# Decoder layer with 32 routed experts: transposes moved into the next expert's first product, the residual split around a product, the overflow branch placed at expert 23

## The chip, the cores and the metric

The kernel runs on one core of one Trainium2 chip. The metric is the device time of one execution in microseconds (us). Of the core's engines this text uses TensorE (PE in the profile, with PEld for its weight loads), VectorE (DVE), ScalarE (ACT), GpSimd (POOL) and SyncE (SP), the queue that issues the large weight transfers.

## What is computed

One decoder layer for 256 tokens of width 1024, in float32: three causal token mixers in parallel, a layer norm, then the part that concerns this change, a top-4-of-32 layer of experts, and a second layer norm on `alpha * x + moe(x)`. The reference, cut to one expert and to the norms:

```python
x = layer_norm(alpha * x + mix(x), ln1_g, ln1_b)

def expert_block(args):
    xb, e = args
    hid = xb @ w_gate_up[e] + b_gate_up[e]          # 1024 -> 2048
    glu = jnp.minimum(hid[:, :D_FF], SWIGLU_LIMIT)
    lin = jnp.clip(hid[:, D_FF:], -SWIGLU_LIMIT, SWIGLU_LIMIT)
    act = glu * jax.nn.sigmoid(SWIGLU_ALPHA * glu) * (lin + 1.0)
    return act @ w_down[e] + b_down[e]              # 1024 -> 1024
...
y = jnp.zeros((t + 1, d)).at[tok_pad].add(y_pad * gate_pad[:, None])[:t]
x = layer_norm(alpha * x + y, ln2_g, ln2_b)
```

Each expert's weights are 12 MB (8 MB up, 4 MB down), so all 32 have to be read once, whatever the routing is.

## The kernel before

After the mixers and the first norm the kernel runs a loop over the experts (line 1317). The first product of expert e, the second product of expert e-1 and the scatter of expert e-2 are written in iteration e, and a scheduler then sets the order of each engine from this program order, the dependences and its own estimates, so that parts of neighbouring iterations can be woven into each other. Only a conditional is a border that nothing is moved over.

**Weights.** `load(e)` issues, on SP's queue, eight pieces of 1 MB for the up weights `wu` of expert e and four for the down weights `wd` of expert e-1. They land in a ring of buffers of 1 MB; a piece can be issued when the product that last used its buffer is done.

**Gather.** Every second iteration `gather` (line 1139) makes the tokens of two experts, `xg`, by 16 matmuls `ps_xg` (line 1152) of one-hot columns `g` with the normed tokens `x`; ACT and DVE copy them out with the gain and shift of the first norm. `spread` (line 1259, POOL) makes `sel`, with which a bias row is added by a matmul.

**First product.** `gemm1` (lines 1163 to 1183) adds the bias to two PSUM tiles `pg` and `pl` (line 1167), then runs over eight pieces k, each four matmuls (line 1171); the scatter of expert e-2 is written behind k = 0. DVE and ACT make `el` from `pg` and `pl` (`eg`, `es` and `el`, lines 1178 to 1182).

**Second product.** `gemm2` (lines 1185 to 1214) transposes `el` in four 128 x 128 blocks (`pt`, line 1188), ACT copies these to `aT` (line 1190); DVE makes the one-hot `gg`, PE transposes it and multiplies it with the gates (`pq`, lines 1197 and 1199), DVE copies `gT` and `gs` out (lines 1203 and 1205). Then comes the bias of `po` (line 1201) and 16 matmuls with the four down pieces (line 1208). ACT makes `oh` and DVE `ol` from `po`, scaled by `gs`.

**Scatter.** `scatter` (lines 1217 to 1224) adds `oh` and `ol`, through `gT`, into four PSUM tiles `y`, which stay open over the whole loop: four matmuls with `oh`, four with `ol`.

**Residual.** The term `alpha * x` of the second norm, with x the output of the first norm, is put into the same four tiles by `residual(h)`, h = 0 and 1 for the halves of the width, in iterations 5 and 6. `lnr` holds the four rows of norm parameters in 32 partitions. `ln_row` spreads a row of it over 128 partitions by four matmuls (`ps_ln`, line 1245); DVE makes `res` from the gain row (line 1234), then adds the shift row (line 1236), and two matmuls with `ident` add `res` into `y` (line 1238). `ps_l` rows of the same form (line 1245) are made for the second norm in the last iterations.

**Conditional.** `IFAT` is 13: in that iteration the loads of expert 14 are issued early, the scatter of expert 12 is put ahead, and a conditional follows that handles experts with more than 64 tokens. In the profiled execution its body is not run; its branch is evaluated on each engine's sequencer.

All PSUM tiles of the tag `misc` (`pt`, `pq`, `ps_ln`, half of the `ps_xg`) share one bank, and `eg`, `es`, `aT`, `oh`, `ol` and `res` share three SBUF buffers of the tag `e3`.

Of the kernel before, what the change touches and what calls it, by code (L numbers as in the profile page):

```python
# [8 lines left out]
F32 = mybir.dt.float32  # L9
# [4 lines left out]
OP = mybir.AluOpType  # L14
# [3 lines left out]
P = 128  # L18
# [5 lines left out]
NRAW, NHL, NA, NB, XB, IFAT, LPP, Y1, Y2, Y3, SG, MG = 3, 3, 4, 3, 1, 13, 1, 3, 3, 3, 4, 2  # L24
ALPHA = 2 ** 0.25
# [8 lines left out]
def tile_layer(ctx, tc, x, xT, memT, w_in, w_convT, a_log, dt_bias, gdn_norm_w, w_mem_kv, w_p_gdn, w_p_sb,  # L34
               w_p_mem, w_o, ln1_g, ln1_b, ln1_T, w_router, b_router, w_gate_up, b_gate_up, w_down, b_down,
               ln2_g, ln2_b, out, dbg=None, cap=CAP, nexp=NE):
    nc = tc.nc
# [15 lines left out]
    V = {}  # L53
# [862 lines left out]
    def begin_gates():  # L916
# [10 lines left out]
        for n, v in enumerate((ln1_g, ln1_b, ln2_g, ln2_b)):  # L927
            nc.gpsimd.dma_start(lnr[8 * n:8 * n + 8, :], v.rearrange("(q c) -> q c", q=8))

# [203 lines left out]
    XG, ACT, SEL, YO = {}, {}, {}, {}  # L1133
# [29 lines left out]
    def gemm1(e, sel, between=None):  # L1163
# [5 lines left out]
        for k in range(KT):  # L1169
# [3 lines left out]
            if k == 0 and between:  # L1173
                between()
# [10 lines left out]
    def gemm2(e, sel, rc, gates):  # L1185
# [14 lines left out]
        po = psg.tile([P, 512], F32, name=f"po{e}", tag="o")  # L1200
        nc.tensor.matmul(po, sel, bias[:, 2, :], start=True, stop=False)  # L1201
# [3 lines left out]
        nc.vector.tensor_copy(gs, pq[:, T:T + 1])  # L1205
        for ft in range(8):
# [18 lines left out]

    def residual(h):

        hs = slice(512 * h, 512 * h + 512)
        res = [ew.tile([P, 512], F32, name=f"res{i}{h}", tag="e3", bufs=3) for i in range(2)]
        for n in range(2):  # L1230
            ps = ln_row(n, h, f"ps_ln{h}{n}")
            for i in range(2):
                if n == 0:
                    nc.vector.scalar_tensor_tensor(res[i], x1[:, i, hs], ALPHA, ps, op0=OP.mult, op1=OP.mult)
                else:
                    nc.vector.scalar_tensor_tensor(res[i], ps, ALPHA, res[i], op0=OP.mult, op1=OP.add)
        for i in range(2):
            nc.tensor.matmul(yps[i][h], ident, res[i], start=False, stop=False, skip_group_check=True)
# [34 lines left out]
    def further_slots():  # L1273
# [16 lines left out]
        with tc.For_i(0, -(-T // cap) - 1, 1):  # L1290
            with tc.For_i(0, nexp, 1) as er:
# [18 lines left out]
                gemm2("o", osel, rc, [gc[:, i:i + 1] for i in range(2)])  # L1310
# [6 lines left out]
    for e in range(nexp + 1):  # L1317
# [3 lines left out]
        if e < nexp:  # L1321
# [3 lines left out]
            gemm1(e, SEL[e], (lambda: scatter(e - 2)) if e - 2 in YO else None)  # L1325
        elif e - 2 in YO:
            scatter(e - 2)
        if e == 1:
            gates_of()
        if e in (5, 6):  # L1330
            residual(e - 5)
        if e == nexp - 1:
            ln2 = ln2_rows()
        if e:
            gemm2(e - 1, SEL[e - 1], rank[:, :, e - 1], [G[:, i, e - 1:e] for i in range(2)])
# [64 lines left out]
```

## Time and profile before

| | us |
|---|---|
| median of three executions | 1317.63 (1315.15 to 1318.44) |
| the profiled execution | 1317.42 |
| its span in the trace | 1315.7 |
| PE busy | 1247.6 (95% of the span) |
| PE weight loads busy | 681.7 (52%) |
| DVE, ACT, POOL busy | 404.3, 278.1, 100.2 |

The span is the time from the first to the last recorded instruction; the profiled execution's own time is 1.7 us longer. Times in the trace are us from the span's start. In the page's table of 40 slices each slice is 32.9 us; the experts begin around the 11th. A row of the timeline gives start, length, engine, line, operation, output and inputs and how many in a row, and in brackets how long the engine had been idle and what released it. Weight loads and matmuls of a float32 product are each recorded as two passes, so the 16 matmuls of a second product appear as 32.

### The profile page before, as it was taken

What the parts mean: (1) busy time and instruction counts of PE and PEld (TensorE: products, weight loads), DVE (VectorE), ACT (ScalarE), POOL (GpSimd) and SP (SyncE); (2) the same over time, 40 slices, a digit from 0 to 9 for tenths busy, and PEclk for the clock granted to TensorE, in tenths of its full rate; (3) what the DMA queues carried; (4) which work ended last, traced back from release to release, by engine and by line L of the source; (5) the groups of instructions that cost most, each with busy time, mean ns of one, the idle gap of its engine ahead of it and who ended that gap; (6) DMA issues with size and microseconds to landing.
All of it is one profiled execution on the core that took longest, in us unless ns stands there. A gap on an engine that the chain in (4) does not pass through costs nothing. (4 is left out here: it accounts for less than half of the span.)

```text
span 1315.7 us, 16784 instructions
## 1 busy us (share of the span) xinstructions
PE 1247.6 (95%) x7023; PEld 681.7 (52%) x7023; DVE 404.3 (31%) x696; ACT 278.1 (21%) x448; POOL 100.2 (8%) x155
## 2 busy tenths in 40 slices
PE   8999999999999998899999999999999999999995
PEld 7998889999734434333333344333333333333342
DVE  6865646557412112111111221111121111111113
ACT  5665636445301101010101011010101011010111
POOL 5223323001000000000000000000000000000001
PEclk9999999999999998799999999999999999999998
DMA  7632347858699999899999979999999999999991
GB/s 241 193 128 89 105 163 232 283 184 300 257 416 423 424 421 425 340 411 407 421 424 421 404 290 422 424 423 422 424 422 425 423 421 424 421 422 425 423 414 49
DMA packets 117135, 453.54 MB, mean 345 GB/s; under 512 B 7440, under 2 KB 47456, under 8 KB 84288
## 3 DMA queue, kind: packets, MB, share of 16 engines
q1 hardware_dynamic: 116096, 450.39, 85.3%
q0 software_dynamic: 960, 2.04, 0.6%
q8 instruction: 57, 0.93, 0.3%
q14 instruction: 22, 0.18, 0.0%
HBM read 451.35 MB, written 1.05 MB: 344 GB/s over the span
## 5 line engine op out<-in xcount | busy, mean ns | idle before, releaser
L1171 PE MATMUL pg<-wu,xg 128*64 128x512 f32 x1024 | 283.6, 600 | 0.0
L1171 PE MATMUL pl<-wu,xg 128*64 128x512 f32 x1024 | 277.8, 593 | 0.0
L1208 PE MATMUL po<-wd,aT 128*64 128x512 f32 x1024 | 240.3, 608 | 0.0
L1178 DVE TENSOR_SCALAR eg<-pg 128x512 f32<-128x512 f32 x32 | 22.1, 692 | 431.9 <-PE pg L1171 431.9
L1171 PEld LDWEIGHTS pl<-wu,xg 128*64 128x64 f32 x1024 | 77.3, 137 | 146.3 <-issue 146.3
L1171 PEld LDWEIGHTS pg<-wu,xg 128*64 128x64 f32 x1024 | 70.5, 136 | 126.5 <-issue 111.6
L1208 PEld LDWEIGHTS po<-wd,aT 128*64 128x64 f32 x1024 | 67.7, 138 | 113.3 <-issue 107.4
L68 ACT ACTIVATE es<-eg 128x512 f32<-128x512 f32 x32 | 20.2, 632 | 463.3 <-DVE eg L1178 463.3
L1214 DVE SCALAR_TENSOR_TENSOR ol<-po,gs,oh 128x512 fp32r<-128x512 f32 x32 | 24.0, 751 | 189.8 <-ACT oh L1213 189.6
L1259 POOL CAST sel<-brs 128x128 fp32r<-128x128 f32 x32 | 11.9, 373 | 880.7 <-PE po L1201 880.1
L1152 PEld LDWEIGHTS ps_xg<-g,x 128*128 128x128 f32 x512 | 61.5, 196 | 28.3 <-issue 27.6
L1152 PE MATMUL ps_xg<-g,x 128*128 128x128 f32 x512 | 68.1, 286 | 0.2 <-DVE g L1141 0.2
L1213 ACT ACTIVATE oh<-po,gs 128x512 fp32r<-128x512 f32 x32 | 22.0, 687 | 218.3 <-PE po L1208 218.3
L1159 ACT ACTIVATE xg<-ps_xg,l1T 128x128 f32<-128x128 f32 x64 | 29.3, 458 | 137.8 <-PE ps_xg L1152 122.4
L1161 DVE TENSOR_SCALAR xg<-ps_xg,l1T 128x128 f32<-128x128 f32 x64 | 26.2, 410 | 90.4 <-ACT xg L1159 89.6
L1223 PE MATMUL y<-oh,gT 64*128 64x512 f32 x128 | 33.8, 461 | 18.8 <-ACT oh L1213 18.0
L1223 PEld LDWEIGHTS y<-oh,gT 64*128 64x128 f32 x128 | 13.3, 184 | 62.0 <-ACT oh L1213 36.5
L1188 PEld LDWEIGHTS pt<-ident,el 128*128 128x128 f32 x128 | 14.4, 146 | 29.2 <-issue 18.1
L1223 PE MATMUL y<-ol,gT 64*128 64x512 f32 x128 | 27.1, 412 | 0.2
L1179 DVE TENSOR_SCALAR el<-pl 128x512 f32<-128x512 f32 x32 | 22.1, 692 | 5.0 <-PE pl L1171 5.0
L1188 PE MATMUL pt<-ident,el 128*128 128x128 f32 x128 | 22.2, 296 | 0.7
L1167 PE MATMUL pl<-bias,sel 128*128 128x512 f32 x32 | 15.7, 492 | 7.2 <-DVE el L1179 7.2
(578 smaller groups left out, 1730.8 us busy)
## 6 DMA issues: line engine op xcount, KB each, us to landing
wu<-in_w_gate_up_dram SPq DMA_DIRECT2D x256, 1024.0 KB, 19.0
wd<-in_w_down_dram SPq DMA_DIRECT2D x127, 1024.0 KB, 19.6
wg<-in_w_in_dram SPq DMA_DIRECT2D x12, 1024.0 KB, 5.8
wo<-in_w_o_dram SPq DMA_DIRECT2D x4, 1024.0 KB, 5.1
wk<-in_w_in_dram SPq DMA_DIRECT2D x2, 1024.0 KB, 6.1
wv<-in_w_in_dram SPq DMA_DIRECT2D x2, 1024.0 KB, 6.0
wsq<-in_w_in_dram SPq DMA_DIRECT2D x2, 1024.0 KB, 5.1
wsk<-in_w_in_dram SPq DMA_DIRECT2D x2, 1024.0 KB, 5.1
```

The lines of the kernel that those rows point to most:

```text
L68: o = nc.scalar.activation(out, in_, func, **kw)
L1152: nc.tensor.matmul(ps[:, k, :], x1[:, i, d * P:(d + 1) * P], g2[:, i].rearrange("p a b -> p (a b)"), start=(i == 0), stop=(i == 1))
L1159: nc.scalar.activation(dst, ps[:, k, :], AF.Identity, scale=g, bias=b)
L1161: nc.vector.tensor_scalar(dst, ps[:, k, :], g, b, op0=OP.mult, op1=OP.add)
L1171: nc.tensor.matmul(ps[64 * h:64 * h + 64, :], XG[e][:, k, :], WU[e][k][:, 512 * c:512 * c + 512], start=False, stop=(k == KT - 1))
L1178: nc.vector.tensor_scalar(g, pg, 7.0, None, op0=OP.min)
L1179: nc.vector.tensor_scalar(l, pl, 7.0, -7.0, op0=OP.min, op1=OP.max)
L1188: nc.tensor.transpose(pt[:, j, :], ACT[e][:, j * P:(j + 1) * P], ident)
L1208: nc.tensor.matmul(po[64 * h:64 * h + 64, :], aT[:, ft % 4, ft // 4, :], WD[e][ft // 2].rearrange("p (a c) -> p a c", a=2)[:, ft % 2, 512 ...
L1213: nc.scalar.activation(oh, po, AF.Copy, scale=gs)
L1214: nc.vector.scalar_tensor_tensor(ol, po, gs, oh.bitcast(F32), op0=OP.mult, op1=OP.subtract)
L1223: nc.tensor.matmul(yps[i][h], gT[64 * h:64 * h + 64, i, :], o[64 * h:64 * h + 64, :], start=(e == 0 and n == 0), stop=(e == nexp - 1 and n ...
```

## The change

- `IFAT` is 23 instead of 13: the early loads, the early scatter and the conditional move to iteration 23.
- The transposes of `el`, the copy `aT`, the transposes `pq` and the copies `gT` and `gs` leave `gemm2` and become `turned(e)`. It is called for expert e-1 within the first product of expert e, behind k = 1; the scatter of expert e-2 stays behind k = 0.
- The residual is split. `residual(h)`, now called ahead of the first product in iterations 5 and 7, makes only the gain row and `res = alpha * x * gain`. `add_residual(h)`, called behind that first product, adds the shift row directly into `y`, by eight matmuls of a new constant `al` (a column of `ident` times alpha, made once on POOL) with `lnr`, and then adds `res` as before.
- The gate values (`gates_of`) are made in iteration 0 instead of 1.

PE, in the gathering iteration of two woven experts, around the second product of the expert before (the rows `po` with `wd`). Before, from the bias of the next first product on:

```order
L1167 MATMUL pg_5438<-bias,sel_5436 128x512
L1167 MATMUL pl_5439<-bias,sel_5436 128x512
L1197 MATMUL pq_5350<-ident,gg_5351 128x128 x2
L1199 MATMUL pq_5350<-G,gg_5351 128x1 x2
L1208 MATMUL po_5357<-wd_0_5281,aT_5348 64x512 x4
L1152 MATMUL ps_xg_5410<-g_12_5407,x_2139 128x128 x7
L1208 MATMUL po_5357<-wd_1_5283,aT_5348 64x512 x4
L1152 MATMUL ps_xg_5410<-g_12_5407,x_2139 128x128
L1208 MATMUL po_5357<-wd_2_5285,aT_5348 64x512 x4
L1188 MATMUL pt_5490<-ident,el_5337 128x128 x4
L1208 MATMUL po_5357<-wd_3_5287,aT_5348 64x512 x4
```

The gather, `pq` and `pt` all stand within the second product. After, the same place:

```order
L1169 MATMUL pg_5442<-bias,sel_5440 128x512
L1169 MATMUL pl_5443<-bias,sel_5440 128x512
L1215 MATMUL po_5365<-wd_0_5285,aT_5320 64x512 x4
L1191 MATMUL pt_5462<-ident,el_5359 128x128 x4
L1215 MATMUL po_5365<-wd_1_5287,aT_5320 64x512 x4
L1215 MATMUL po_5365<-wd_2_5289,aT_5320 64x512 x4
L1215 MATMUL po_5365<-wd_3_5291,aT_5320 64x512 x4
```

Only `pt` of the following expert has stayed there. What left it stands within the first product of the same pair (rows `pg` and `pl` with `wu`), between its pieces. After:

```order
L1230 MATMUL y_3824<-ol_5266,gT_5211 128x512
L1200 MATMUL pq_5322<-ident,gg_5323 128x128 x2
L1173 MATMUL pg_5295<-wu_1_5271,xg_5148 64x512 x2
L1173 MATMUL pl_5296<-wu_1_5271,xg_5148 64x512 x2
L1202 MATMUL pq_5322<-G,gg_5323 128x1 x2
L1212 MATMUL po_5365<-bias,sel_5175 128x512
L1154 MATMUL ps_xg_5414<-g_12_5411,x_2139 128x128 x3
L1173 MATMUL pg_5295<-wu_2_5273,xg_5148 64x512 x2
L1173 MATMUL pl_5296<-wu_2_5273,xg_5148 64x512 x2
L1154 MATMUL ps_xg_5414<-g_12_5411,x_2139 128x128 x5
```

The transposes `pq` now surround piece 1, and the gather's first rows `ps_xg` come behind them and around piece 2.

PE in iteration 5, first half of the residual. Before, behind the last piece of the first product (`wu_7`):

```order
L1171 MATMUL pl_4461<-wu_7_4448,xg_4313 64x512 x2
L1167 MATMUL pg_4625<-bias,sel_4623 128x512
L1167 MATMUL pl_4626<-bias,sel_4623 128x512
L1245 MATMUL ps_ln_4521<-lnr,ident 128x128 x4
L1238 MATMUL y_3819<-res_4512,ident 128x512
L1238 MATMUL y_3821<-res_4513,ident 128x512
L1188 MATMUL pt_4530<-ident,el_4388 128x128 x4
L1197 MATMUL pq_4537<-ident,gg_4538 128x128 x2
L1199 MATMUL pq_4537<-G,gg_4538 128x1 x2
L1208 MATMUL po_4544<-wd_0_4450,aT_4535 64x512 x4
```

The shift row, the two residual matmuls, `pt` and `pq` follow each other between two products. After, within the first product of iteration 5:

```order
L1191 MATMUL pt_4491<-ident,el_4408 128x128 x3
L1248 MATMUL y_3821<-lnr,al 128x128 x4
L1200 MATMUL pq_4498<-ident,gg_4499 128x128 x2
L1202 MATMUL pq_4498<-G,gg_4499 128x1 x2
L1173 MATMUL pg_4471<-wu_2_4440,xg_4315 64x512 x2
L1173 MATMUL pl_4472<-wu_2_4440,xg_4315 64x512 x2
L1248 MATMUL y_3823<-lnr,al 128x128 x4
L1251 MATMUL y_3821<-res_4467,ident 128x512
L1173 MATMUL pg_4471<-wu_3_4442,xg_4315 64x512 x2
L1173 MATMUL pl_4472<-wu_3_4442,xg_4315 64x512 x2
L1251 MATMUL y_3823<-res_4468,ident 128x512
```

The `lnr,al` matmuls and the residual matmuls have moved between the pieces of the product; the gain row `ps_ln` (not among these rows) stands in the second product ahead of it.

The diff, cut to what matters:

```diff
-NRAW, NHL, NA, NB, XB, IFAT, LPP, Y1, Y2, Y3, SG, MG = 3, 3, 4, 3, 1, 13, 1, 3, 3, 3, 4, 2
+NRAW, NHL, NA, NB, XB, IFAT, LPP, Y1, Y2, Y3, SG, MG = 3, 3, 4, 3, 1, 23, 1, 3, 3, 3, 4, 2
...
+        V["al"] = al = ctile([32, 8], "al", pool=mo2)
+        nc.gpsimd.tensor_scalar(al, ident[0:32, 8:16], ALPHA, None, op0=OP.mult)
...
-            if k == 0 and between:
-                between()
+            if k < len(between):
+                between[k]()
...
-    def gemm2(e, sel, rc, gates):
+    def turned(e, rc, gates):
+
         pt = psg.tile([P, 4, P], F32, name=f"pt{e}", tag="misc")
...
-        po = psg.tile([P, 512], F32, name=f"po{e}", tag="o")
-        nc.tensor.matmul(po, sel, bias[:, 2, :], start=True, stop=False)
         gT = ew.tile([P, 2, P], F32R, name=f"gT{e}", tag="gT", bufs=1)
         nc.vector.tensor_copy(gT.rearrange("p i t -> p (i t)"), pq[:, :T])
         gs = ew.tile([P, 1], F32, name=f"gs{e}", tag="gs")
         nc.vector.tensor_copy(gs, pq[:, T:T + 1])
+        TU[e] = aT, gT, gs
+
+    def gemm2(e, sel):
+        aT, gT, gs = TU.pop(e)
+        po = psg.tile([P, 512], F32, name=f"po{e}", tag="o")
+        nc.tensor.matmul(po, sel, bias[:, 2, :], start=True, stop=False)
...
     def residual(h):
 
         hs = slice(512 * h, 512 * h + 512)
-        res = [ew.tile([P, 512], F32, name=f"res{i}{h}", tag="e3", bufs=3) for i in range(2)]
-        for n in range(2):
-            ps = ln_row(n, h, f"ps_ln{h}{n}")
-            for i in range(2):
-                if n == 0:
-                    nc.vector.scalar_tensor_tensor(res[i], x1[:, i, hs], ALPHA, ps, op0=OP.mult, op1=OP.mult)
-                else:
-                    nc.vector.scalar_tensor_tensor(res[i], ps, ALPHA, res[i], op0=OP.mult, op1=OP.add)
-        for i in range(2):
-            nc.tensor.matmul(yps[i][h], ident, res[i], start=False, stop=False, skip_group_check=True)
+        ps = ln_row(0, h, f"ps_ln{h}")
+        RES[h] = [ew.tile([P, 512], F32, name=f"res{i}{h}", tag="e3", bufs=3) for i in range(2)]
+        for i in range(2):
+            nc.vector.scalar_tensor_tensor(RES[h][i], x1[:, i, hs], ALPHA, ps, op0=OP.mult, op1=OP.mult)
+
+    def add_residual(h):
+
+        for i in range(2):
+            for q in range(4):
+                r = 4 * h + q
+                nc.tensor.matmul(yps[i][h][:, q * P:(q + 1) * P], V["al"][:, r:r + 1].to_broadcast([32, P]), lnr,
+                                 start=False, stop=False, skip_group_check=True)
+        for i in range(2):
+            nc.tensor.matmul(yps[i][h], ident, RES[h][i], start=False, stop=False, skip_group_check=True)
...
-            gemm1(e, SEL[e], (lambda: scatter(e - 2)) if e - 2 in YO else None)
-        elif e - 2 in YO:
+            if e in (5, 7):
+                residual((e - 5) // 2)
+            between = [lambda: scatter(e - 2)] if e - 2 in YO else []
+            if e:
+                between.append(lambda: turned(e - 1, rank[:, :, e - 1], [G[:, i, e - 1:e] for i in range(2)]))
+            gemm1(e, SEL[e], between)
+            if e in (5, 7):
+                add_residual((e - 5) // 2)
+        else:
             scatter(e - 2)
-        if e == 1:
+            turned(e - 1, rank[:, :, e - 1], [G[:, i, e - 1:e] for i in range(2)])
+        if e == 0:
             gates_of()
-        if e in (5, 6):
-            residual(e - 5)
...
-            gemm2(e - 1, SEL[e - 1], rank[:, :, e - 1], [G[:, i, e - 1:e] for i in range(2)])
+            gemm2(e - 1, SEL[e - 1])
```

## Rows read from the trace of the kernel before

**Rows 1.** Page, parts 1 and 2: engines' busy us; 40 slices, clock in tenths, GB/s.
```profile
PE 1247.6 (95%) x7023; PEld 681.7 (52%) x7023; DVE 404.3 (31%) x696; ACT 278.1 (21%) x448; POOL 100.2 (8%) x155
...
PEclk9999999999999998799999999999999999999998
...
GB/s 241 193 128 89 105 163 232 283 184 300 257 416 423 424 421 425 340 411 407 421 424 421 404 290 422 424 423 422 424 422 425 423 421 424 421 422 425 423 414 49
```

**Rows 2.** Waits of PE, 800 to 1280: us in total, times, longest.
```profile
PE y L1223 <- ACT oh L1213: 11.0, 13, 0.8
PE pl L1167 <- DVE el L1179: 4.1, 14, 0.3
PE pg L1167 <- POOL sel L1259: 1.7, 2, 0.9
```

**Rows 3.** Timeline of PE, the scatters' second halves (others between left out).
```profile
402.97 0.62 PE L1223 MATMUL y<-ol,gT 64*128 64x512 f32 x4
...
428.31 0.63 PE L1223 MATMUL y<-ol,gT 64*128 64x512 f32 x4
...
457.22 0.62 PE L1223 MATMUL y<-ol,gT 64*128 64x512 f32 x4
...
595.28 0.94 PE L1223 MATMUL y<-ol,gT 64*128 64x512 f32 x4
...
622.00 0.95 PE L1223 MATMUL y<-ol,gT 64*128 64x512 f32 x4
...
654.19 0.95 PE L1223 MATMUL y<-ol,gT 64*128 64x512 f32 x4
```

**Rows 4.** Timeline of PE, second products, at 901 and in the last iterations.
```profile
901.17 5.37 PE L1208 MATMUL po<-wd,aT 128*64 128x512 f32 x24
...
1254.12 1.15 PE L1245 MATMUL ps_l<-lnr,ident 32*128 32x128 f32 x8
1255.21 1.94 PE L1208 MATMUL po<-wd,aT 128*64 128x512 f32 x8
```

**Rows 5.** Timeline of PE at the residual's first half.
```profile
500.89 1.25 PE L1245 MATMUL ps_ln<-lnr,ident 32*128 32x128 f32 x8 [1.62 <-DVE res L1234]
...
502.93 3.78 PE L1238 MATMUL y<-res,ident 128*128 128x512 f32 x4 [0.78 <-DVE res L1236]
```

**Rows 6.** Windows: us, busy PE, PEld, DVE, ACT, POOL; PEclk, DMA share, GB/s.
```profile
496.00:504.00 8.00, 4.93 (x20) 2.18 (x17) 5.16 (x8) 0.63 (x1) 0.00 (x0) 0.86 1.01 419
504.00:512.00 8.00, 7.32 (x20) 3.52 (x20) 0.82 (x3) 0.59 (x1) 0.00 (x0) 0.50 1.03 429
544.00:552.00 8.00, 7.11 (x18) 3.84 (x20) 1.58 (x5) 0.59 (x1) 0.00 (x0) 0.50 0.76 323
552.00:560.00 8.00, 8.00 (x28) 2.31 (x26) 0.00 (x0) 0.00 (x0) 0.00 (x0) 0.72 0.52 184
752.00:760.00 8.00, 6.87 (x36) 2.62 (x34) 3.17 (x6) 1.10 (x2) 0.00 (x0) 1.00 0.41 165
760.00:768.00 8.00, 6.58 (x43) 3.69 (x39) 1.94 (x4) 0.85 (x2) 0.00 (x0) 1.00 0.20 61
1288.00:1296.00 8.00, 7.11 (x37) 2.75 (x35) 1.24 (x3) 1.16 (x2) 0.00 (x0) 1.00 0.01 2
```

**Rows 7.** Timeline of PE and of DVE around a first product's end.
```profile
1251.21 0.49 PE L1167 MATMUL pl<-bias,sel 128*128 128x512 f32 x1 [0.30 <-DVE el L1179]
...
1282.78 0.42 DVE L1203 CAST gT<-pq 128x256 fp32r<-128x256 f32 x1 [0.48 <-PE pq L1199]
1283.12 0.68 DVE L1182 TENSOR_TENSOR el<-el,es 128x512 f32<-128x512 f32 x1
```

**Rows 8.** Waits of SP, 735 to 775, and timeline of PE, there and at the end.
```profile
SPq L829 <- PEq L1340: 7.8, 1, 7.8
...
754.81 0.44 PE L1197 MATMUL pq<-ident,gg 128*128 128x128 f32 x2 [1.13 <-ACT aT L1190]
...
1293.83 7.09 PE L1208 MATMUL po<-wd,aT 128*64 128x512 f32 x32
```

More of the change, by code (lines that the diff above doesn't have):

```diff
@@ L1132, in tile_layer @@
     yps = [[psy.tile([P, 512], F32, name=f"y{i}{dh}", tag=f"y{i}{dh}") for dh in range(2)] for i in range(2)]
-    XG, ACT, SEL, YO = {}, {}, {}, {}
+    XG, ACT, SEL, TU, YO = {}, {}, {}, {}, {}
     def load(e):
@@ L1161, in gather, with gemm1 @@
                     nc.vector.tensor_scalar(dst, ps[:, k, :], g, b, op0=OP.mult, op1=OP.add)
-    def gemm1(e, sel, between=None):
+    def gemm1(e, sel, between=()):
         pg = psg.tile([P, 512], F32, name=f"pg{e}", tag="glu")
@@ L1224, in scatter @@
                                      start=(e == 0 and n == 0), stop=(e == nexp - 1 and n == 1), skip_group_check=True)
+    RES = {}
     def residual(h):
         hs = slice(512 * h, 512 * h + 512)
-        res = [ew.tile([P, 512], F32, name=f"res{i}{h}", tag="e3", bufs=3) for i in range(2)]
-        for n in range(2):
-            ps = ln_row(n, h, f"ps_ln{h}{n}")
-            for i in range(2):
-                if n == 0:
-                    nc.vector.scalar_tensor_tensor(res[i], x1[:, i, hs], ALPHA, ps, op0=OP.mult, op1=OP.mult)
-                else:
-                    nc.vector.scalar_tensor_tensor(res[i], ps, ALPHA, res[i], op0=OP.mult, op1=OP.add)
-        for i in range(2):
-            nc.tensor.matmul(yps[i][h], ident, res[i], start=False, stop=False, skip_group_check=True)
+        ps = ln_row(0, h, f"ps_ln{h}")
+        RES[h] = [ew.tile([P, 512], F32, name=f"res{i}{h}", tag="e3", bufs=3) for i in range(2)]
+        for i in range(2):
+            nc.vector.scalar_tensor_tensor(RES[h][i], x1[:, i, hs], ALPHA, ps, op0=OP.mult, op1=OP.mult)
[7 more added lines that the diff above has]
+            nc.tensor.matmul(yps[i][h], ident, RES[h][i], start=False, stop=False, skip_group_check=True)
     def ln_row(n, h, name):
@@ L1309, in further_slots @@
                 WD["o"] = [down_piece("o", k, er) for k in range(4)]
-                gemm2("o", osel, rc, [gc[:, i:i + 1] for i in range(2)])
+                turned("o", rc, [gc[:, i:i + 1] for i in range(2)])
+                gemm2("o", osel)
                 scatter("o")
```

## The prediction

> **What bounds the kernel now.** I read the page first. TensorE (PE) is busy for 95% of the span, and the 40 slices tell the stages apart: from the 12th slice on, the experts, the DMA moves 421 to 425 GB/s in nearly every slice. Two slices stand out: the 17th (340 GB/s), where the granted clock also falls to 0.7, and the 24th (290 GB/s) [rows 1]. In the expert stage PE and DMA are close. Two experts need 24 pieces of 1.049 MB, 25.17 MB, so 59.6 us at 422 GB/s. PE needs 58.9 us, as the marks below show. Which of the two binds is told by the waits: in 480 us of the stage PE waits 11.0 us for the scaled copy `oh`, 4.1 us for `el`, 1.7 us for `sel`, and the list ends there [rows 2]. No weight load of it waits for a DMA. So PE binds, and the pieces arrive just in time.
>
> Next the marks: each end of a scatter on PE is a beat, one expert apart [rows 3]. 402.97 to 428.31 to 457.22 is 25.3 and 28.9 us, 54.3 a pair: experts not woven into each other. 595.28 to 622.00 to 654.19 is 26.7 and 32.2, 58.9 a pair: the woven order of most experts. Between, four beats from 457.22 to 595.28 take 138.1 us. They hold the residual.
>
> **The residual's split.** What would four beats cost without it? The orders around them: 25.3 + 32.2 + 26.7 + 32.2 = 116.4 us. So the residual costs 21.7 us today. What is in that? Its own PE work: a group of eight `ps_l` rows goes from 1254.12 to 1255.21, 1.09 us [rows 4]; four of these are 4.4. The eight residual matmuls took 3.78 us for four at half clock [rows 5], so some 0.45 each at full clock, 3.6 for all eight. Stalls: PE stands 1.62 us before the second row group and 0.78 before the residual matmuls, each for DVE's `res` [rows 5]; twice, 4.8. The rest, 21.7 - 4.4 - 3.6 - 4.8 = 8.9, is the clock: behind the stalls it is granted at 0.50, once for each half (504 to 512 and 544 to 552), and as PE frees slots late, the DMA drops to 323 and 184 GB/s [rows 6].
>
> After the change `ps_ln` is formed once a half and handed to DVE; PE then has pieces k2 and k3 to multiply and the `lnr,al` matmuls to do before it needs `res`, as the order shows. Work: two row groups of 1.09 (2.2), sixteen `lnr,al` matmuls, which are as long as four such groups (4.4), and the same eight residual matmuls (3.6): 10.1. Around each half some four cuts of the product: eight weight-and-multiply steps in a row take 1.94 us and 24 take 5.37 [rows 4], so 0.214 each and 0.22 for a fresh start; eight cuts are 1.6. For waits I leave 2.0, one of the 0.3 to 0.8 us kind per group. That is 13.7 in place of 21.7, **-8.0**. The bounds: nothing of the waits and cuts, -11.6; all the stalls come back but not the clock, -4. I take -8.0, since the stall rows are both waits for DVE work that now runs under 3.5 us or more of product per half.
>
> **Experts not woven** (four at the start, four behind the conditional, before and after alike). The first product of one expert now begins right after the second of another, with the old 0.84-us wait for `sel` [rows 2] covered by the gather or gone; in exchange `pt` and `pq` cut the product at three places, 0.66. About -0.15 each, **-1.2**; bounds 0 and -3 (from -0.84 + 0.44).
>
> **The woven experts**, ten pairs. Per pair PE runs the same matmuls. The second product loses the cuts by the gather and `pq`; the first product gets them: I count nine cuts before and nine after. What could be new is a wait. First, `pt` now stands behind only `pl`'s bias and one down piece (0.49 + 1.94 us) after DVE's first `el` step; DVE needs two more steps of one size, 0.68 each [rows 7], so it is ready with about 1 us to spare: nothing. Second, the gather's `ps_xg` now follows `pq` and waits till DVE has copied `gT` (0.42 [rows 7]) and the one column `gs` out of the same bank, with only a bias matmul (as `pl`'s, 0.49) between: with two hand-overs some 0.2 us per pair. The wait for `oh` (0.84) stays where it is. So **+2.0**; the bounds are cuts saved at two places, -0.4 a pair, and a full copy exposed in both experts, +1.1: -4 to +11.
>
> **The conditional at 23 instead of 13.** On PE its stretch costs 1.13 us, where `pq` waits for the copy `aT` that was just made [rows 8]. After the change `aT` is made during the first product, so this last goes: **-1.0**, bounds 0 and -2.5. The DMA is what suffers: SP drains its queue, waits 7.8 us for PE's branch [rows 8], and the DMA falls to 165 and 61 GB/s [rows 6]; against 422 these are 8 x 0.61 + 8 x 0.86 = 11.7 us of rest. PE did not wait for it. Moving the rest to expert 23 costs nothing if the ring of slots covers it there too. The cover: from the conditional to the end the DMA runs full, 421 to 425 GB/s [rows 1], and yet its last bytes came by about 1288, while the last second product began at 1293.83, took 7.09 [rows 6, 8] and so reached its last quarter 5.3 us later. There is some 11 us of cover left at the end, and the same sum of rests and short beats lies ahead of it after the change. I cost it at nothing; if the cover were gone, it would be +8 to +12.
>
> **The end.** The last first product has the same 1.13-us pattern; **-0.5**.
>
> Sum: -8.0 - 1.2 + 2.0 - 1.0 - 0.5 = -8.7. The profiled execution took 1317.42 us (span 1315.7), 0.2 under the median of 1317.63, so nothing is to be corrected: 1317.4 - 8.7 = **1308.7, said 1309**.
>
> **Rivals.**
>
> R1, slower: the moved transposes expose a wait at every expert. `pt`, its copy `aT`, `pq` and `gT` pass from PE to ACT to PE to DVE to PE, and each hand-over that is not covered is worth what `oh` costs now, 0.84 us [rows 2]. If one such wait appears in each of 28 experts, that is +23.5 against -8.7 and the time is 1332. It decides from 8.7/28 = 0.31 us per expert. For it: four hand-overs lie in one product, and all PSUM tiles named `misc` share one bank. Against it: a down or up piece is 1.9 us, longer than any of the copies, and the order leaves one between nearly all of them.
>
> R2, no change: the clock falls again. The two residual blocks still put transposes, `lnr,al` and `pq` matmuls beside each other, and if the clock drops to half as now, the 8.9 us return: 1317.6. For it: in the trace the fall to 0.50 begins in the stretch with those small matmuls. Against it: the fall stands behind a stretch with only 4.9 of 8 us busy [rows 6], and every later expert has `pt` and `pq` without a fall (from the 19th slice on, 9 throughout [rows 1]).
> The Trainium skill ("TensorE: Matmul & The Clock Gate", section "Part 4: PE-mode transpose") says that transposes do not count as PE activity for the clock the way matmuls do. That speaks against a change that sets transposes beside the residual; by it the time would be R2's, and by the rows of the later experts, with as many transposes and a clock of 1.00, it would be the forecast's. It gives R2 its chance.
>
> R3, cheaper: no new waits, cuts saved, stalls of the residual all gone: -11.6 - 3 - 4 is 1299 at best; I take 1301.
>
> R4, the DMA binds and not PE. Then PE's gains count for nothing and only the DMA's rests do: at the residual 8 x (1 - 323/422) + 8 x (1 - 184/422) = 1.9 + 4.5 = 6.4 us go, the 11.7 at the conditional stay: 1311. For it: the DMA needs 59.6 us a pair, PE 58.9. Against it: [rows 2].
> The skill ("Perfetto Trace Analysis", section "Identifying the Most-Contended Engine") holds that the matmul busy share is a poor measure and the weight loads' share a better one; that share is 52% here [rows 1], which would make the DMA the bound and R4 the answer. The waits of the trace disagree: PE stops for no transfer.
>
> R5: expert 23 has less cover than 13, and PE starves by the rest's 8 to 12 us: 1317 to 1321.
>
> **How the numbers follow.** Chances: the forecast 0.52, R4 0.06 (beside it, 1311), R3 0.13, R2 0.11, R5 0.05, R1 0.13. A measurement of this kernel can tell about 0.3%, 4 us, from no change: faster is below 1313.7, slower above 1321.6. Faster: forecast, R4 and R3 less 0.02 of the forecast's upper edge, 0.69. Same: R2, R5 and that edge, 0.18. Slower: R1, 0.13. The range has to take in R3, the forecast and R2: 1299 to 1319; left out are R1, the dear half of R5 and a little below.
>
> **What would show it.** In the trace of the changed kernel: the four beats around iterations 5 to 8 sum to about 130 us, the granted clock stays near 1.00 there, and the DMA does not fall below 400 GB/s; waits for `res` are under 1 us. The `pt` and `ps_xg` rows of woven experts carry waits of 0 and 0.2 us, and a pair takes 59.1. At expert 23 SP again waits about 8 us for PE's branch, the DMA rests about 12 us and PE's weight loads do not wait. Waits of PE for `aT` or `gT` of 0.3 us and more at each expert would prove R1; a clock of 0.50 in iteration 5 or 7, R2; waits of PE for `wu` or `wd`, R4 or R5.

## The result and the profile after

The changed kernel takes 1331.1 us (median of four, 1329.21 to 1332.9) against 1318.04 for the kernel before on the same chip: 1.0101 times as long, 95% interval 1.0077 to 1.0125. It is 13 us slower, where 9 us faster had been predicted. The profiled execution's span is 1328.9 us.

The page of the changed kernel, parts 1, 2 and 6 (as in [rows 1]; of part 6 the line of the up weights, with KB each and us from issue to landing):

```profile
PE 1262.2 (95%) x7039; PEld 682.1 (51%) x7039; DVE 400.3 (30%) x692; ACT 276.8 (21%) x448; POOL 99.8 (8%) x156
...
PEclk9999999999999999999999999999999999999998
...
GB/s 238 177 142 74 117 135 224 305 191 289 258 418 422 424 422 423 421 413 415 422 420 419 422 424 424 421 423 422 422 423 424 263 389 422 425 421 424 423 278 32
...
wu<-in_w_gate_up_dram SPq DMA_DIRECT2D x256, 1024.0 KB, 10.3
```

The same line of the kernel before:

```profile
wu<-in_w_gate_up_dram SPq DMA_DIRECT2D x256, 1024.0 KB, 19.0
```

The dip of clock and transfers in the 17th slice is gone, and the one of the conditional has moved from the 24th to the 32nd. A piece lands 10.3 us after its issue; before it took 19.0. So fewer pieces are under way at a time, and it is PE that is late.

Waits of PE, 800 to 1280, changed kernel (us in total, times, longest; before: [rows 2]):

```profile
PE y L1230 <- ACT oh L1220: 11.0, 13, 0.8
PE pg L1169 <- PEq L1360: 4.0, 1, 4.0
PE pl L1169 <- DVE el L1181: 3.5, 12, 0.3
PE ps_xg L1154 <- DVE gs L1206: 1.7, 5, 0.3
```

Two of these lines are new: 4.0 us behind the branch, and 0.3 for each gather. (A fifth, `ps_l` with 0.3, belongs to the end, below.) They are far from 13 us. The beats tell the rest. Timeline of PE, changed kernel, scatters (as in [rows 3]):

```profile
406.56 0.62 PE L1230 MATMUL y<-ol,gT 64*128 64x512 f32 x4
...
432.27 0.62 PE L1230 MATMUL y<-ol,gT 64*128 64x512 f32 x4
...
461.55 0.63 PE L1230 MATMUL y<-ol,gT 64*128 64x512 f32 x4
...
592.20 0.95 PE L1230 MATMUL y<-ol,gT 64*128 64x512 f32 x4
...
619.18 0.95 PE L1230 MATMUL y<-ol,gT 64*128 64x512 f32 x4
...
651.80 0.95 PE L1230 MATMUL y<-ol,gT 64*128 64x512 f32 x4
```

With all marks of both traces the span can be cut into stretches that answer to each other:

| stretch (us) | before | after | difference |
|---|---|---|---|
| up to the first mark | 402.97 | 406.56 | +3.6 |
| two beats, not woven | 54.25 | 54.99 | +0.7 |
| four beats with the residual | 138.06 | 130.65 | -7.4 |
| seventeen woven beats | 498.39 | 504.05 | +5.7 |
| five beats around and behind the conditional | 143.04 | 149.37 | +6.3 |
| from the last woven mark to the last mark | 65.83 | 70.10 | +4.3 |
| behind it | 13.16 | 13.18 | 0.0 |

The residual came out as predicted (130.65 against "about 130"), and four other stretches took it back with 17.0 us. The first line of the table is another matter. Up to the first row of the gather (351.80 before, 355.89 after) the programs are the same but for one small POOL instruction; in the traces of the twelve kernels of this study this row begins anywhere from 351.8 to 357.6, and the trace of before is the earliest of them. So the late start is not the change's, and from the gather on the changed kernel is 9.1 us longer in this pair of traces. What is missing to 13 lies with the residual: before, its four beats took 138.06 us in this trace, and the same code took 132.3 to 134.8 in three others (below). Against those the difference would be some 12 to 15 us, an estimate.

The end, timeline of PE, changed kernel, from 1276 on (all of its waits in the last first product, and the first behind it):

```profile
1276.98 0.90 PE L1258 MATMUL ps_l<-lnr,ident 32*128 32x128 f32 x6 [0.34 <-DVE gs L1206]
...
1280.83 0.93 PE L1258 MATMUL ps_l<-lnr,ident 32*128 32x128 f32 x6 [0.68 <-ACT ln L1266]
...
1284.72 0.71 PE L1258 MATMUL ps_l<-lnr,ident 32*128 32x128 f32 x4 [0.68 <-ACT ln L1266]
...
1288.60 0.48 PE L1258 MATMUL ps_l<-lnr,ident 32*128 32x128 f32 x2 [0.68 <-ACT ln L1266]
...
1297.71 0.66 PE L1191 MATMUL pt<-ident,el 128*128 128x128 f32 x4 [0.60 <-DVE el L1184]
```

Before, the `ps_l` rows stood in four whole groups between the down pieces of a second product and waited for nothing [rows 4]. Now they stand behind `pq` in a first product, share its bank, and are cut into pieces of two to six. These rows and the `pt` behind them wait 0.34 + 3 x 0.68 + 0.60 = 3.0 us. One more wait is laid bare: the scatter behind that second product, before and after:

```profile
1264.06 0.73 PE L1223 MATMUL y<-oh,gT 64*128 64x512 f32 x3
```

```profile
1270.05 0.73 PE L1230 MATMUL y<-oh,gT 64*128 64x512 f32 x3 [0.84 <-ACT oh L1220]
```

Before, the last `ps_l` group stood ahead of this scatter, and `oh` was ready when PE came to it. With 3.0 and 0.84 added and the old 1.13 for `aT` gone, waits make up 2.7 of the 4.3 us. The rest is put down to the cuts; that was not measured apart.

### The profile page after: what moved, and what is told of

It reads as the page before. It is cut to its first block, busy times and chain, and to the rows that moved or that the text cites. A ratio compares the mean times of both kernels' runs of the same rounds, so it can differ in the third digit from the quotient of the medians.

```text
span 1328.9 us, 16802 instructions
## 1 busy us (share of the span) xinstructions
PE 1262.2 (95%) x7039; PEld 682.1 (51%) x7039; DVE 400.3 (30%) x692; ACT 276.8 (21%) x448; POOL 99.8 (8%) x156
## 5 line engine op out<-in xcount | busy, mean ns | idle before, releaser
L1173 PE MATMUL pg<-wu,xg 128*64 128x512 f32 x1024 | 316.3, 604 | 0.0
L1173 PE MATMUL pl<-wu,xg 128*64 128x512 f32 x1024 | 306.8, 593 | 0.0
L1215 PE MATMUL po<-wd,aT 128*64 128x512 f32 x1024 | 231.7, 597 | 0.0
L1173 PEld LDWEIGHTS pl<-wu,xg 128*64 128x64 f32 x1024 | 86.6, 137 | 145.8 <-issue 145.7
L1215 PEld LDWEIGHTS po<-wd,aT 128*64 128x64 f32 x1024 | 68.8, 136 | 127.3 <-issue 117.3
L1173 PEld LDWEIGHTS pg<-wu,xg 128*64 128x64 f32 x1024 | 75.7, 136 | 106.0 <-issue 87.5
L1204 DVE CAST gT<-pq 128x256 fp32r<-128x256 f32 x32 | 13.6, 424 | 147.2 <-PE pq L1202 147.2
L1193 ACT COPY aT<-pt 128x512 f32<-128x512 f32 x32 | 18.6, 580 | 46.5 <-PE pt L1191 46.5
L1191 PEld LDWEIGHTS pt<-ident,el 128*128 128x128 f32 x128 | 13.4, 140 | 28.2 <-DVE xg L1163 9.7
## 6 DMA issues: line engine op xcount, KB each, us to landing
wu<-in_w_gate_up_dram SPq DMA_DIRECT2D x256, 1024.0 KB, 10.3
```

The lines of the kernel that those rows point to most:

```text
L1173: nc.tensor.matmul(ps[64 * h:64 * h + 64, :], XG[e][:, k, :], WU[e][k][:, 512 * c:512 * c + 512], start=False, stop=(k == KT - 1))
L1193: nc.scalar.copy(aT.rearrange("p j a b -> p j (a b)"), pt)
L1215: nc.tensor.matmul(po[64 * h:64 * h + 64, :], aT[:, ft % 4, ft // 4, :], WD[e][ft // 2].rearrange("p (a c) -> p a c", a=2)[:, ft % 2, 512 ...
```

## Experiments

The theory after the result: each of the three parts has its own price, the moved transposes and the moved conditional cost, the split gains. The rivals: the DMA paces the pairs (59.60 us, the sum of 26.98 and 32.62, is what 24 pieces need at 422 GB/s); the conditional costs only beside the moved transposes; the split's gain is lost further on. The first four kernels take the parts singly.

**The conditional alone at 23.**

```diff
-NRAW, NHL, NA, NB, XB, IFAT, LPP, Y1, Y2, Y3, SG, MG = 3, 3, 4, 3, 1, 13, 1, 3, 3, 3, 4, 2
+NRAW, NHL, NA, NB, XB, IFAT, LPP, Y1, Y2, Y3, SG, MG = 3, 3, 4, 3, 1, 23, 1, 3, 3, 3, 4, 2
```

> The kernel before with one number changed: the conditional stands at expert 23 instead of 13. Nothing else moves. The changed kernel's trace shows 4.0 us of idle PE behind the branch at 23, where the kernel before showed 0.53 behind the branch at 13, and the six beats around the conditional are 6.3 us longer. Theory A (the later place itself costs, since the code behind the branch or the drained queue is met differently there): about +4 to +6 us on the kernel before, with an idle PE of about 4 us behind the branch. Theory B (the place costs nothing, the moved transposes beside it do): within 1.5 us of the kernel before, idle PE behind the branch 0.5 to 1 us. The prediction's own figure for the move alone was 0, with the DMA's cover as the only danger.

Measured: 1322.68 us, ratio 1.0042 (1.0023 to 1.0062), 5.5 us slower. Timeline of PE at the branch:

```profile
1060.46 0.77 PE L1167 MATMUL pg<-bias,sel 128*128 128x512 f32 x1 [3.57 <-PEq L1340]
```

The five beats there take 148.3 us, 5.3 more than at 13. Theory A so far: the move costs by itself, and not by the transposes.

**The changed kernel with the conditional at 13.** 
```diff
-NRAW, NHL, NA, NB, XB, IFAT, LPP, Y1, Y2, Y3, SG, MG = 3, 3, 4, 3, 1, 23, 1, 3, 3, 3, 4, 2
+NRAW, NHL, NA, NB, XB, IFAT, LPP, Y1, Y2, Y3, SG, MG = 3, 3, 4, 3, 1, 13, 1, 3, 3, 3, 4, 2
```

> The changed kernel with the conditional back at expert 13. Theory A (the later place costs): 4 to 6 us less than the changed kernel, so about 1325 to 1327. Theory B (it does not): as the changed kernel, about 1331, and idle PE of several us behind the branch at 13 as well.

Measured: 1326.58 us, ratio 1.006 (1.0036 to 1.0085), with 0.5 us idle behind the branch. Against the changed kernel's 1.0101 that is 0.41% or 5.4 us, the same as the conditional alone. Its price adds to the others.

**The split alone.** `residual` ahead of `gemm1` and `add_residual` behind it in iterations 5 and 7, with `al`, all else as before.

```diff
...
+            if e in (5, 7):
+                residual((e - 5) // 2)
             gemm1(e, SEL[e], (lambda: scatter(e - 2)) if e - 2 in YO else None)
+            if e in (5, 7):
+                add_residual((e - 5) // 2)
...
-        if e in (5, 6):
-            residual(e - 5)
```

> The kernel before with the residual's split alone: gain row and product with x ahead of the first product in iterations 5 and 7, shift row by matmuls with the constant and the residual matmuls behind it; transposes and conditional as before. Theory A (the split does what the prediction said, and all the loss comes from the other two parts): the four beats of the residual about 130 us in place of 138, no fall of the granted clock there, and 7 to 8 us less than the kernel before, about 1310. Rival: the gain is given back further on, because the DMA needs 59.6 us for two experts and becomes the bound as soon as PE is earlier: 0 to 3 us less than before, with waits of PE's weight loads for transfers near the end.

Measured: 1311.11 us, ratio 0.9957 (0.9941 to 0.9973), 5.7 us faster. The four beats take 127.9 us (460.46 to 588.37), PE waits for no `res`, and the granted clock is 1.00 throughout. The gain reaches the end, so the DMA didn't take it back.

**The moved transposes alone.** Against the changed kernel (`residual` is the old function again):

```diff
-NRAW, NHL, NA, NB, XB, IFAT, LPP, Y1, Y2, Y3, SG, MG = 3, 3, 4, 3, 1, 23, 1, 3, 3, 3, 4, 2
+NRAW, NHL, NA, NB, XB, IFAT, LPP, Y1, Y2, Y3, SG, MG = 3, 3, 4, 3, 1, 13, 1, 3, 3, 3, 4, 2
...
-            if e in (5, 7):
-                residual((e - 5) // 2)
...
-            if e in (5, 7):
-                add_residual((e - 5) // 2)
...
+        if e in (5, 6):
+            residual(e - 5)
```

> The kernel before with the moved transposes alone: residual unsplit in iterations 5 and 6, conditional at 13. Theory A (cuts and one wait per pair make each pair of experts longer on PE): woven pairs 59.6 us in place of 58.9, pairs not woven 55.0 in place of 54.3, the last two beats 4 us longer for the rows of the second norm that now stand in a first product; in all 10 to 13 us more than the kernel before, about 1329, with PE waiting for no transfer. Rival: 59.6 us is the rate of the transfers, so the pairs are paced by the DMA; then PE's weight loads wait for transfers, a piece takes about 20 us to land, and pieces are not issued late by PE.

Measured: 1327.47 us, ratio 1.0083 (1.006 to 1.0107), 10.9 us slower. Woven beats of 26.98 and 32.62, others of 25.8 and 29.3, the last stretch 70.1 us: as in the changed kernel. No wait of PE for a transfer. So far as foreseen; what was not is the residual. Its four beats, unsplit, take 131.2 us (463.09 to 594.26), no more than with the split in the changed kernel (130.65). Timeline of PE there:

```profile
507.62 1.94 PE L1213 MATMUL po<-wd,aT 128*64 128x512 f32 x8
509.92 1.15 PE L1250 MATMUL ps_ln<-lnr,ident 32*128 32x128 f32 x8 [0.35 <-DVE res L1239]
511.00 1.07 PE L1213 MATMUL po<-wd,aT 128*64 128x512 f32 x2
512.00 1.98 PE L1243 MATMUL y<-res,ident 128*128 128x512 f32 x4
```

With `pt` and `pq` gone from the head of the second product, a down piece came to stand ahead of the second row group; the stall is 0.35 in place of 1.62, the next is gone, the clock stays at 1.00 (1.98 us for the four residual matmuls that took 3.78, [rows 5]). Moved transposes and split mend the same stall. Beside the former the latter is worth 0.5 us in beats, 0.9 in medians (1327.47 to 1326.58) and 3.0 by the ratios (1.0083 and 1.006), whose intervals overlap: less than the 5.7 it has alone, and not told from nothing.

**What in the conditional's place costs?** Two other places, again with the kernel before; in the second the number is 25.

```diff
-NRAW, NHL, NA, NB, XB, IFAT, LPP, Y1, Y2, Y3, SG, MG = 3, 3, 4, 3, 1, 13, 1, 3, 3, 3, 4, 2
+NRAW, NHL, NA, NB, XB, IFAT, LPP, Y1, Y2, Y3, SG, MG = 3, 3, 4, 3, 1, 21, 1, 3, 3, 3, 4, 2
```

> The kernel before with the conditional at expert 21. Theory A (a later place costs as such): 3 to 4 us of idle PE behind the branch, as at 23. Theory C (what costs is whether the code behind the skipped body has been fetched when the branch is taken; at 23 a 16 KB instruction transfer falls between the branch and the first matmul behind it, at 13 it had come before): idle PE at 21 is about 0.5 us if no instruction transfer lies in that gap, and 3 to 4 us if one does, whatever the number of the expert. Beside it, the four residual beats of the same code once more: before, two executions took 138.1 and 132.3 us.

> The kernel before with the conditional at expert 25. As at 21: theory A says 3 to 4 us of idle PE behind the branch; theory C says 0.5 us without and 3 to 4 us with an instruction transfer in the gap. The four residual beats a further time, 132 to 138 us if the length of the clock's fall differs from one execution to the next.

Measured, one execution each: 1319.91 and 1321.33 us. Timelines of PE, first at 21, then at 25:

```profile
1000.30 0.47 PE L1167 MATMUL pg<-bias,sel 128*128 128x512 f32 x1 [0.56 <-PEq L1340]
1000.61 0.60 PE L1152 MATMUL ps_xg<-g,x 128*128 128x128 f32 x4
1003.19 4.54 PE L1152 MATMUL ps_xg<-g,x 128*128 128x128 f32 x28 [1.98 <-issue]
```

```profile
1120.95 0.76 PE L1167 MATMUL pg<-bias,sel 128*128 128x512 f32 x1 [3.50 <-PEq L1340]
```

At 25 the wait is as at 23. At 21 the branch itself costs 0.56 as at 13, but five rows later PE stands for 1.98 us and waits for nothing that the profile shows. The five beats take 146.4 and 148.0 us, 3.4 and 4.9 more than at 13. DMA of the changed kernel in its gap (1060.4 to 1064.4; queue and kind, packets, MB, share), of the kernel with 25 in its own (1117.5 to 1121), and of the kernel with 21 from the branch to the end of its second stop (999.7 to 1003.2):

```profile
q8 instruction: 1, 0.02, 2.2%
```

```profile
q8 instruction: 1, 0.02, 1.7%
```

```profile
q8 instruction: 1, 0.02, 1.7%
```

In the first two the only packet that moves is one of instructions; the kernel with 23 alone has the same in its gap. At 21 weights move too, and the instruction packet begins at 1000.66, ahead of the stop of 1.98 us. In the kernel before, at 13, no packet of this queue comes between 757 and the branch; one had come at 755 to 757. The page counts 57 of them with 0.93 MB, so 16 KB each.

This parts all twelve traces. In each of them a packet begins 0.9 to 1.1 us behind the last matmul ahead of the branch. In the eight where PE waits 0.5 to 0.6 us, the packet before that one had begun 6 to 11 us ahead of the branch; in the four with a long stop (at 21, 23 twice, 25) it had begun 20 to 23 us ahead, and PE goes on 2.5 to 3.1 us after the start of the new one. The profile doesn't say which engine's instructions a packet holds.

To tell the place from the fetch, the code at 23 was pushed on by 63 transposes with their weight loads: one small transpose of iteration 2 is done 64 times. That is about half a packet, if the 57 packets hold the 14046 matmuls and weight loads that the page counts (an estimate).

```diff
-        nc.tensor.transpose(ps[:1, :P], rmx, ident)
+        for _ in range(64):
+            nc.tensor.transpose(ps[:1, :P], rmx, ident)
```

> The kernel before with the conditional at 23, and one small transpose in iteration 2 done 64 times over; these are extra instructions on PE, some 128 with their weight loads, which push all later instructions on by half of a 16 KB instruction transfer. They cost 5 to 15 us by themselves. Theory C (the wait behind the branch is for instructions not yet fetched): the wait changes, from 3.6 us to about 0.5, or splits up as at 21, and the instruction transfer no longer lies in the gap. Theory A (the place as such): 3.5 us of idle PE behind the branch as in the unshifted kernel.

Measured, one execution: 1320.01 us, of which the extra transposes take 6.9 (beat of 32.2 in place of 25.3). Timeline of PE behind the branch at 23, and the instruction packets of 1055 to 1056.5, 5 us ahead of it:

```profile
1062.74 0.47 PE L1167 MATMUL pg<-bias,sel 128*128 128x512 f32 x1 [0.64 <-PEq L1341]
```

```profile
q8 instruction: 1, 0.02, 4.4%
```

The wait is 0.64, the beat with the branch takes 32.07 (31.97 at 13), and the packet came before the branch. So the number of the expert is not what costs. PE is stopped when the code behind the skipped body isn't there yet, and whether it is depends on where the branch falls in the stream of packets. The Trainium skill ("Runtime: NRT & Kernel Launch", section "Instruction fetch mechanics") says as much: instructions are fetched in blocks of 16 KB, in sequence and ahead of need, and a taken branch to a block that isn't held waits for its transfer. The traces agree, with 3.5 to 4.0 us for it. A second cost follows it. Windows of the changed kernel (columns as in [rows 6]):

```profile
1056.00:1064.00 8.00, 3.49 (x18) 1.03 (x14) 1.18 (x2) 0.69 (x1) 0.00 (x0) 0.89 0.01 3
1064.00:1072.00 8.00, 7.61 (x40) 6.58 (x42) 2.42 (x6) 1.77 (x4) 0.00 (x0) 0.69 0.84 330
```

Behind the idle stretch the granted clock is 0.69 on the mean of 8 us; at 13 it stayed at 1.00 [rows 6]. The gather stands in it. Timeline of PE, the kernel with 23 alone, then the kernel before:

```profile
1061.03 5.70 PE L1152 MATMUL ps_xg<-g,x 128*128 128x128 f32 x32
```

```profile
765.81 3.73 PE L1152 MATMUL ps_xg<-g,x 128*128 128x128 f32 x32
```

So of the 5.3 us that the place costs 3.0 are the longer wait and 2.0 the slower gather.

**The cuts.** In the beats that are not woven, `pq` stands after the first step of piece k2. Timeline of PE, with one row of ACT, changed kernel:

```profile
434.69 0.66 PE L1191 MATMUL pt<-ident,el 128*128 128x128 f32 x4
435.28 1.07 PE L1173 MATMUL pg<-wu,xg 128*64 128x512 f32 x2
435.38 0.58 ACT L1193 COPY aT<-pt 128x512 f32<-128x512 f32 x1 [5.36 <-PE pt L1191]
436.28 0.44 PE L1200 MATMUL pq<-ident,gg 128*128 128x128 f32 x2
...
446.06 1.45 PE L1173 MATMUL pl<-wu,xg 128*64 128x512 f32 x3
447.43 0.49 PE L1212 MATMUL po<-bias,sel 128*128 128x512 f32 x1
```

The lone step (two passes) holds PE for 1.00 us, from 435.28 to 436.28; two passes within a run take 0.43 (0.214 each, from [rows 4]). It is not `aT`, out of the bank that `pq` shares, that `pq` waits for: the copy ended at 435.96, and where `pq` does wait for one it starts 0.06 us behind its end (754.75 and 754.81 in the kernel before). To see what that is worth, `pq` got a callback of its own behind k = 2, so that both cuts fall between whole pieces; conditional at 13, split as in the change.

```diff
+        TU[e] = aT
+
+    def turned_gates(e, rc, gates):
+        aT = TU[e]
         pq = psg.tile([P, 512], F32, name=f"pq{e}", tag="misc")
...
                 between.append(lambda: turned(e - 1, rank[:, :, e - 1], [G[:, i, e - 1:e] for i in range(2)]))
+                between.append(lambda: turned_gates(e - 1, rank[:, :, e - 1], [G[:, i, e - 1:e] for i in range(2)]))
```

> The changed kernel with the conditional at 13 and the moved work called in two parts, pt and its copy behind k = 1, pq and its copies behind k = 2, so that pq no longer falls within a piece. In the pairs that are not woven a single step of piece k2 stands between pt and pq and takes 1.00 us where two such passes take 0.43 elsewhere. Theory (a cut within a piece leaves one half of the array unpaired and costs 0.4 to 0.6 us, a cut between pieces 0.1 to 0.2): beats that are not woven 0.4 us shorter each (28.9 and 25.4 in place of 29.3 and 25.8), woven pairs as before at 59.6, in all 3 us less than the changed kernel with the conditional at 13. Rival (what costs is the number of cuts, wherever they are): no difference.

Measured: 1317.04 us, ratio 0.9991 (0.9974 to 1.0008); against 1.006 for the same kernel with the cut piece that is 9 us less, three times what was expected. Its marks and a piece between two cuts:

```profile
819.31 0.63 PE L1233 MATMUL y<-ol,gT 64*128 64x512 f32 x4
...
822.33 1.08 PE L1173 MATMUL pg<-wu,xg 128*64 128x512 f32 x4
823.23 1.03 PE L1173 MATMUL pl<-wu,xg 128*64 128x512 f32 x4
824.19 0.44 PE L1203 MATMUL pq<-ident,gg 128*128 128x128 f32 x2
...
832.68 1.03 PE L1173 MATMUL pl<-wu,xg 128*64 128x512 f32 x4
833.63 0.51 PE L1215 MATMUL po<-bias,sel 128*128 128x512 f32 x1
...
844.29 0.63 PE L1233 MATMUL y<-ol,gT 64*128 64x512 f32 x4
```

The beat is 24.98 (25.82 with the cut piece), the other kind 28.44 (29.28): 0.84 each, twice the estimate. The ends of the products show why: behind a cut within a piece the steps of the two halves pair up one place on, and so the last step of the product is alone as well. Its last four passes take 1.37 us (446.06 to 447.43) in the changed kernel and 0.95 (832.68 to 833.63) here, 0.42 more, about as much as the lone step ahead of `pq`. The first woven beat of a pair fell too, from 26.98 to 26.74, its length in the kernel before, which was not expected: there `pq` now stands behind piece 2 together with the bias of `po`, in one cut in place of two. So a cut between whole pieces is worth 0.24. In beats this is 6.9 us from first to last mark; 1.8 of the span are the stretch ahead of the first mark.

**The residual's form or its place?** Both rows by DVE as before, in the new place, no matmuls with `al`. Against the kernel before (`add_residual` keeps the two residual matmuls, `residual` the rest):

```diff
...
-        for i in range(2):
-            nc.tensor.matmul(yps[i][h], ident, res[i], start=False, stop=False, skip_group_check=True)
+    def add_residual(h):
+
+        for i in range(2):
+            nc.tensor.matmul(yps[i][h], ident, RES[h][i], start=False, stop=False, skip_group_check=True)
...
+            if e in (5, 7):
+                residual((e - 5) // 2)
             gemm1(e, SEL[e], (lambda: scatter(e - 2)) if e - 2 in YO else None)
+            if e in (5, 7):
+                add_residual((e - 5) // 2)
...
-        if e in (5, 6):
-            residual(e - 5)
```

> The kernel before with the residual in its old form (both rows by DVE, no shift row by matmul) but in the new place: rows and DVE work ahead of the first product in iterations 5 and 7, the residual matmuls behind it. Theory (the place is what helps, DVE's work runs under the product): residual beats 126 to 129 us, no fall of the clock, as much under the kernel before as the split alone, 5 to 8 us, and perhaps 1 to 2 more since eight row matmuls take the place of sixteen. Rival (the form is what helps: half of the work of DVE): stalls of 0.8 to 1.6 us and a fall of the clock return, 132 us and more, 0 to 3 us under the kernel before.

Measured: 1309.2 us, ratio 0.9927 (0.9904 to 0.995), 9.6 us faster. Timeline of PE, first half:

```profile
490.30 1.15 PE L1250 MATMUL ps_ln<-lnr,ident 32*128 32x128 f32 x8 [0.32 <-DVE res L1236]
...
494.97 1.99 PE L1243 MATMUL y<-res,ident 128*128 128x512 f32 x4
```

The four beats take 126.2 us, 1.7 less than with the shift row by matmuls. The place alone gives the whole gain. DVE's second pass is hidden by the product but for 0.32 us a half, and sixteen row matmuls in place of eight are a cost without a return. (The new form in the old place was not run.)

**Put together.** Conditional at 13, residual in the old form at the new place, transposes within the first product, in whole pieces, only for the experts that are not woven. Against the kernel with whole pieces, beside the residual:

```diff
-            if e:
+            if e in (1, 2, 3, 4, 14, 15, 16):
...
         if e:
+            if e - 1 not in TU:
+                turned(e - 1, rank[:, :, e - 1], [G[:, i, e - 1:e] for i in range(2)])
+                turned_gates(e - 1, rank[:, :, e - 1], [G[:, i, e - 1:e] for i in range(2)])
             gemm2(e - 1, SEL[e - 1])
```

> What the runs point to, put together: conditional at 13, residual in its old form in the new place, and the transposes called within the first product, in whole pieces, only in the iterations whose experts are not woven (1 to 4 and 14 to 16); elsewhere they stay in the second product. Expected from the beats measured apart: residual 126 us as with the place alone, beats that are not woven 28.44 and 24.9 in place of 28.91 and 25.35 (0.45 each, seven of them, 3 us), woven pairs 58.9 as before. In all 9 to 13 us under the kernel before, about 1306. Rival: the DMA, 59.6 us a pair, binds now that PE is ahead; then PE's weight loads wait for transfers near the end and the time stays at 1309 or more.

Measured: 1308.44 us, ratio 0.9931 (0.9911 to 0.9951), 9.1 us faster than before and no faster, within the intervals, than the place alone. The beats that are not woven are 28.44 and 24.9 to 25.0 as expected, woven pairs 58.9; the residual's beats took 127.3, 1.1 of the 3 us back. PE's weight loads wait for no transfer from 1200 to the end, so the DMA doesn't bind yet.

## Why the prediction was wrong

Four steps failed. The residual's split was priced against one execution and added as if the moved transposes left its stall in place. A cut within a piece was priced like one between pieces. The move of the conditional was costed at nothing. And the rows that give way at the end were not looked at.

**What bounds the kernel** was right. In every kernel run here PE sets the time, and no trace shows it waiting for a transfer in the experts. R4 and R5 are out; in the changed kernel a piece even lands 8.7 us sooner after its issue. Only the sentence "No weight load of it waits for a DMA" goes too far. Waits of PE's weight loads, kernel before, 800 to 1280 (us in total, times, longest), two of the lines:

```profile
PEld pg L1171 <- issue: 58.3, 201, 0.4
...
PEld pg L1171 <- DMA wd<-in_w_down_dram: 4.8, 16, 0.4
```

In all 23 gaps, 6.6 us, are put down to transfers. They are no longer than the gaps of the same rows that wait for nothing, and no matmul of PE waits for a transfer in that time, so the conclusion stands.

**The residual** was right in its mechanism and wrong as a term. Split, it took 130.65 us of a predicted 130.1, with the clock at 1.00. But the 138.1 that it was set against was one execution's. The same code ahead of the conditional took 132.3, 134.8 and 134.8 us in the traces with the conditional at 23, 21 and 25: how long the clock stays low after the same stalls differs. Windows of the kernel with the conditional at 23, for [rows 6]:

```profile
504.00:512.00 8.00, 6.54 (x26) 3.71 (x28) 2.07 (x5) 0.59 (x1) 0.00 (x0) 0.79 1.04 429
...
544.00:552.00 8.00, 6.54 (x21) 3.24 (x22) 2.11 (x5) 0.59 (x1) 0.00 (x0) 0.64 1.01 427
```

0.79 and 0.64 in place of 0.50 twice. So the gain was 5.7 alone, not 8.0. The second fault is heavier: the terms were added as if independent. The moved transposes had already taken the stall away, so that within the change the split is worth 0.5 us in beats, and no run tells it from nothing. That the four beats came to the predicted figure is partly luck: the split alone took 127.9, 2.2 less than the working gives, and the moved transposes lengthen the beats around it.

**Experts not woven:** -0.15 a beat predicted, +0.4 measured, since a cut in the middle of a piece was priced like one between pieces, 0.22, where it leaves two steps alone, 0.84. The wait for `sel` did go. In whole pieces the same move gives -0.4 to -0.5.

**Woven experts:** +0.2 a pair predicted, +0.7 measured (5.7 us over seventeen beats). The wait of the gather for `gs` was found and is 0.34, not 0.2; the wait of `pt` is nothing, as reckoned. The second beat of a pair is 0.44 longer, which is that wait and 0.1. The first is 0.24 longer, and that is the one cut that `pq` makes between pieces 1 and 2, as the whole-piece kernel shows, where it is gone; the count "nine cuts before and nine after" missed it. The bounds held the sum.

**The conditional:** -1.0 predicted for its stretch, and the 1.13 us for `aT` did go: the beat ahead of the branch takes 23.0 us in place of 24.1. But the move to 23 was costed at nothing, and it costs 5.3 to 5.5. The step that failed is "On PE its stretch costs 1.13 us", which has no term for the branch itself, and the search for danger in the weights' DMA alone. The trace of before had 0.53 us of PE waiting for its own sequencer behind the branch, and its page listed 57 instruction packets; that a jump lands in code that has yet to come was not thought of, and no bound had it.

**The end:** -0.5 predicted, +4.3 measured. The 1.13-us wait did go, but the `ps_l` rows were pushed from a second product into the last first product, where they wait for ACT, and what they had covered, a wait for `oh`, lay open. A step that looked only at what the change moves, not at what gives way to it, missed them.

**The rivals.** R1 named 1332 us, and the time is 1331, but by accident: PE waits nowhere for `aT` or `gT`, and the new wait for `gs` comes once a pair. R2 is out: `pt`, `pq` and the `lnr,al` matmuls stand beside each other with the clock at 1.00 throughout, so the rule of the Trainium skill on transposes ("TensorE: Matmul & The Clock Gate", section "Part 4: PE-mode transpose") does not show as a cause here; in the experts the clock fell behind idle PE, at the residual of before and behind the branch. By ratios the whole is 10.9 (transposes) + 5.5 (conditional) - 3.0 (split beside them) = 13.4, against 13 measured; each of these terms is uncertain by some 3 us.

## What to carry to other kernels

Where the engine that binds is already busy, moving its work between two products is no gain in itself: price each cut by where it falls in the neighbour, keep it between whole pieces, and look at what the scheduler pushes aside. Two edits that mend one stall don't add up, so take the parts of a change one at a time. And before a stall is priced from one trace, look whether a second execution shows it as long.

## What the runs showed of the hardware

A branch over a body that is not run cost 0.5 to 0.6 us, or 3.5 to 4.0 us and a slower clock behind it (0.56 and 1.98 in one case), by where it fell between 16 KB packets of instructions: the last one had begun 6 to 11 us ahead of it in the cheap cases, 20 to 23 in the dear ones. 63 extra transposes with their weight loads ahead of it removed the wait. A lone matmul step on half of the columns (two passes) holds PE for 1.00 us; in a run of such steps, which use the two halves by turns, the same two passes take 0.43; and a cut there leaves the last step of the product alone too. The fall of the granted clock after equal stalls (1.62 and 0.78 us) had not the same length in every execution: 138.1, 132.3, 134.8 and 134.8 us for the same four beats.
